# Attention's PSUM banks and the layout of its transposed probabilities, in a hybrid encoder layer

## The chip, the cores and the metric

One core of one Trainium2 chip runs the whole layer as one program. The metric is device time of one execution in microseconds; lower is better. The kernel before takes 2172.15 us, the median of three runs (2170.88 to 2173.38).

## What is computed

One layer over 2048 positions of width 1024. The first half normalises the input, projects it to 1280 columns and splits these among three mixers: a bidirectional diagonal state-space scan (S5), a two-dimensional Fourier mixer, and windowed attention. Their outputs are concatenated, projected, normalised, gated and added to the input. The second half is a gated MLP with a convolution of width 3 between its two products. The change touches attention alone:

```python
def window_attention(q, k, v, sink):
    # 6 query heads, 2 key/value heads of 64; blocks of 128 queries see the 128 keys
    # before, at and after them: kb, vb = band(k), band(v), 384 positions a block
    ...
    scores = jnp.einsum('bnqkgd,bnskd->bnkgqs', qb, kb).astype(jnp.float32) + bias
    ...
    m = jnp.maximum(jnp.max(scores, axis=-1, keepdims=True), sink_l)
    p = jnp.exp(scores - m)
    p = p / (jnp.sum(p, axis=-1, keepdims=True) + jnp.exp(sink_l - m))
    out = jnp.einsum('bnkgqs,bnskd->bnqkgd', p.astype(v.dtype), vb)
    return out.reshape(bsz, seq, ATT_WIDTH)
```

## The kernel before

**Numbers.** Products are made in float16 with each operand split in a high and a low half (HI, LO). A product is then three matmuls: high by high, low by high, high by low (`mm3`). TensorE writes into PSUM, which has eight banks of 128 partitions by 512 float32. The program divides the banks into three pools, `PTAGS`: z has three, s has four, m has one.

**Order of the work.** Every part of the layer is a Python generator. A small planner (`Sched`) runs all of them against modelled clocks: a generator asks for an engine and a duration, or for banks of a pool (`"acq"`), or waits for another's result (`"w"`), and the planner always serves the request that can start first by its model; among those that wait for banks, the one with the lower priority number is looked at first. What comes out is one fixed order of instructions for each engine. On the chip the engines run these orders one instruction after the other; semaphores hold an instruction until its inputs are there. DMAs are issued by SyncE (SP), in order as well. Scratch tiles come from one rotating set of 50 buffers (`u`).

**Who uses which pool around attention.** The S5 chain uses s before attention. The Fourier mixer, the GLU behind S5, the projections of queries (`q_tile`) and the output projection (`proj`) use z. A query tile of chunks 1 to 3 asks for one bank of z with two more to spare, so for a z that is wholly free. The norms' sums over partitions use m. The MLP takes banks of s and z; its first product takes one bank of s as soon as its first weights are there and then waits for its operand.

**Attention** (`att`, L1275 on). The 16 blocks of 128 queries are numbered 0 to 15; four make a chunk of 512 positions (chunks 0 to 3, `c`). Two workers, both instances of the same generator, take the even and the odd blocks, so a pair of blocks (`hb`) is in work at once. Worker 0 loads queries, keys and values of the pair (nine DMAs), once chunk `c`'s query tiles have been stored. The score bank and all other banks of attention come from pool s for chunks 0 and 1, from pool z for chunks 2 and 3 (`bt`). A block goes through these steps:

1. For each of six heads: two score matmuls into a bank, then one VectorE instruction that adds the bias and takes the maximum (L1332).
2. Softmax: maxima with the sink, six exponentials on ScalarE with their sums, reciprocal (L1346) and scale.
3. For each of three pairs of heads: both heads' probabilities are scaled and split into high (ScalarE) and low (VectorE) halves; then they are transposed in 128 by 128 pieces by matmuls against an identity, four pieces to a bank, and each bank is evacuated in one instruction of 512 columns. Of three banks of a pair, ScalarE evacuates two and VectorE one.
4. The output product into one bank: 64 partitions for each of the two value heads, 128 columns for each of its three query heads. As a pair of heads shares a buffer and the middle pair belongs to two value heads, there are four groups of columns: 256, 128, 128 and 256 wide.
5. ScalarE and VectorE evacuate the high and the low half of the output into `ya`, and `f_ya[n]` is set.

**What waits for attention.** The output projection of chunk `c` waits for the four blocks of the chunk. It makes eight tiles of 24 matmuls; each is evacuated by ScalarE twice, once scaled by a constant column (`proj_evac`). Behind it `post` normalises, adds the residual, stores it and prepares the MLP's input. The MLP's first operands are made by `hcomb(0)`, which waits for `f_ya[15]`, the last block.

Nearly all instructions are issued from helpers, so their lines in the profile are the helpers': L318 matmul, L272 ScalarE activation, L277 tensor_tensor, L284 tensor_scalar on VectorE, L291 scalar_tensor_tensor, L267 DMA.

Of the kernel before, what the change touches and what calls it, by code (L numbers as in the profile page):

```python
# [10 lines left out]
F16 = mybir.dt.float16  # L11
I32 = mybir.dt.int32
AF = mybir.ActivationFunctionType
ALU = mybir.AluOpType
X = mybir.AxisListType.X

P = 128
# [20 lines left out]
HI, LO = 0, 1  # L38
# [164 lines left out]
class Builder:  # L203
    UNITS = 50
    PTAGS = {"z": 3, "s": 4, "m": 1}
    LAT = 0.12
    ATT_SLACK = (0.0, 10.0)
    NORM_SLACK = 2.0
    PE_TR = 4
    ATT1 = 0  # L210

    def __init__(self, tc, ctx, A, O):
# [1064 lines left out]
    def att(self, worker):  # L1277

        V, PE, SP = self.V, self.PE, self.SP
        for hb in range(8):  # L1280
            c = hb // 2
            bt = "s" if c < 2 else "z"
            b0, b1 = max(2 * hb - 1, 0), min(2 * hb + 3, 16)
            if worker == 0 and hb % 2 == 0:
                if c == 1 and ATT_GATE:
# [3 lines left out]
            if worker == 0:  # L1289
# [5 lines left out]
                Q, K, VV = self.u([6, 256], F16), self.u([2, 2, 512], F16), self.u([2, 4, P], F16)  # L1295
                t0, nb = hb * 256, b1 - b0
                for x in range(2):
                    for kv in range(2):
                        r = slice(64 * kv, 64 * kv + 64)
                        t = yield from self.dma(ta, Q[64 * x:64 * x + 64, 3 * kv:3 * kv + 3],  # L1300
                                                self.qd[:, r, x, t0:t0 + 256].rearrange("j p t -> p j t"))
                for x in range(2):
                    r = slice(64 * x, 64 * x + 64)
                    for kv in range(2):
                        t = yield from self.dma(ta, K[r, kv, :, :nb * P],
                                                self.kd[:, kv, :, b0 * P:b1 * P].rearrange("x p t -> p x t"))
                t = yield from self.dma(ta, VV[:, :, :nb], self.vd[:, :, b0:b1])
                self.f_q[hb].set(t, (Q, K, VV))
            tq = yield ("w", self.f_q[hb])
            Q, K, VV = self.f_q[hb].val  # L1310
            ya = self.yatt[c]
            n = 2 * hb + worker
            k0, k1 = max(n - 1, 0), min(n + 1, 15)
            nk = k1 - k0 + 1
            bo = (k0 - n + 1) * 128
            st = self.cpool.tile([P, 6, 6], F32, tag="soft", name=self.nm("st"), bufs=4)
            mx, nm, es, r, dn, sm = (st[:, i] for i in range(6))
            sb = []
            tt_ = []
            for h in range(6):  # L1320
                kv = h // 3
                tb = yield ("acq", self.bank[bt], 1)
                ps = self.ps(bt)
                o = ps[:, :nk * 128]
                if h % 2 == 0:
                    sb.append(self.u([2, 384]))
                t = yield from self.mm(max(tb, tq), [(o, Q[:, h, worker * 128:worker * 128 + 128],
                                                      K[:, kv, x, (k0 - b0) * P:(k1 + 1 - b0) * P], x == 0, x == 1)
                                                     for x in range(2)])
                s_ = sb[h // 2][:, h % 2, :nk * 128]  # L1330
                t = yield ("V", 0.08 + 0.00105 * nk * 128, t)
# [4 lines left out]
            t = yield from self.tt(t, mx, mx, self.sink, ALU.max)  # L1336
# [3 lines left out]
            for h in range(6):  # L1340
                s_ = sb[h // 2][:, h % 2, :nk * 128]
                t = yield from self.act(tn, s_, s_, AF.Exp, scale=1.0 / 256, bias=nm[:, h:h + 1],
                                        accum_out=sm[:, h:h + 1])
            t = yield from self.tt(t, dn, sm, es, ALU.add)
            t = yield ("V", 0.1, t)
            V.reciprocal(r, dn)  # L1346
            tr = yield from self.ts(t, r, r, SW, None, ALU.mult)
            pts, tps = [], []
            for g in range(3):
                pp, dd = self.u([2, 2, 384], F16), self.u([2, 2, nk, P], F16)  # L1350
                tp = []
                for j in range(2):
                    h = 2 * g + j
                    s_ = sb[g][:, j, :nk * 128]
                    ph, pl = pp[:, HI, j, :nk * 128], pp[:, LO, j, :nk * 128]
                    t = yield from self.act(tr, ph, s_, AF.Copy, scale=r[:, h:h + 1])
                    t1 = yield from self.stt(t, pl, s_, r[:, h:h + 1], ph, ALU.mult, ALU.subtract)
                    tp.append(t1)
                    if c >= self.PE_TR:
                        for x, src, tx in ((HI, ph, t), (LO, pl, t1)):  # L1360
                            t = yield ("Q", 1.2, tx)
                            SP.dma_start_transpose(out=dd[:, x, j], in_=src)
                        tps_ = t + 2.2 + self.ATT_SLACK[c > 0]
                if c < self.PE_TR:
                    df = dd.rearrange("p x j k q -> p (x j k) q")
                    blk = [(x, j, k) for x in range(2) for j in range(2) for k in range(nk)]
                    for i in range(0, 4 * nk, 4):
                        tb = yield ("acq", self.bank[bt], 1)
                        ps = self.ps(bt)
                        t = yield from self.mm(max(tb, tp[1]), [  # L1370
                            (ps[:, e * P:(e + 1) * P], pp[:, x, j, k * P:(k + 1) * P], self.id16f, True, True)
                            for e, (x, j, k) in enumerate(blk[i:i + 4])])
                        if i % 8 == 0:
                            t = yield from self.act(t, df[:, i:i + 4], ps.rearrange("p (a b) -> p a b", a=4), AF.Copy)
                        else:
                            t = yield from self.ts(t, df[:, i:i + 4], ps.rearrange("p (a b) -> p a b", a=4), 1.0, None, ALU.mult)
                        self.free(t, ps)
                        tps_ = max(t, tps_) if i else t
                pts.append(dd)
                tps.append(tps_)  # L1380
            tb = yield ("acq", self.bank[bt], 1)
            po = self.ps(bt)
            for g, j0, nj in ((0, 0, 2), (1, 0, 1), (1, 1, 1), (2, 0, 2)):
                kv, c0 = divmod(2 * g + j0, 3)
                o = po[64 * kv:64 * kv + 64, c0 * 128:(c0 + nj) * 128].rearrange("p (a b) -> p a b", a=nj)
                cv = slice(64 * kv, 64 * kv + 64)
                t = max(tb, tps[g])
                for k in range(nk):
                    t = yield from self.mm3(t, o, (VV[:, HI, k0 - b0 + k, cv], VV[:, LO, k0 - b0 + k, cv]),
                                            (pts[g][:, HI, j0:j0 + nj, k], pts[g][:, LO, j0:j0 + nj, k]),  # L1390
                                            k == 0, k == nk - 1)
            ql = (n % 4) * 128
            pv = po[:, 0:384].rearrange("p (a b) -> p a b", a=3)
            t = yield from self.act(t, ya[HI][:, :, ql:ql + 128], pv, AF.Copy, scale=1.0 / SW)
            t = yield from self.stt(t, ya[LO][:, :, ql:ql + 128], pv, 1.0 / SW, ya[HI][:, :, ql:ql + 128],
                                    ALU.mult, ALU.subtract)
# [722 lines left out]
```

## Time and profile before

| | |
|---|---|
| median of three runs | 2172.15 us |
| the profiled execution | 2173.84 us |
| its span, first to last instruction | 2172.1 us |
| instructions | 27409 |
| TensorE, VectorE, ScalarE busy | 91%, 72%, 46% of the span |
| mean granted TensorE clock | 0.96 of full speed |
| attention, first score evacuation to last | 466.9 to 839.9 us |

The page of the profile gives busy time by engine, then the span in 40 slices of 54.3 us, in which a digit is a share in tenths. Matmul times overlap, so a busy TensorE is not one at its peak, and the granted clock says at what rate it ran. A row of grouped instructions reads: line, engine, operation, output and inputs, shapes, count, then busy time, mean duration in ns, and the idle time before them with what ended it. A row of the timeline gives start, duration, engine, line, operation and the number of merged instructions. `ps` is a PSUM bank, `u` a scratch buffer, `c` a constant, `st` the softmax columns, `d` a buffer in HBM.

### The profile page before, as it was taken

Reading aid. Unit: us, or ns where it says so; the run is one execution under the profiler, and the core shown is the slowest. Engines: PE = TensorE matmul, PEld = TensorE weight load, DVE = VectorE, ACT = ScalarE, POOL = GpSimd, SP = SyncE. Lnnn points to the kernel's source line nnn. Section 1 sums busy time; section 2 is a strip of 40 time slices with the busy share of each in tenths; the row PEclk is TensorE's granted clock in tenths of the full one; section 3 lists DMA queues with packets and bytes.
Section 4 is the critical chain, followed back from the end, with each engine's and each line's share of the span. In section 5 each row is a group of like instructions: output and inputs, shape, how many; then the busy total and the mean of one; then the engine's idle time right before and its main releaser. Section 6 shows DMA issues by size and latency. Waiting matters only on the chain.

```text
span 2172.1 us, 27409 instructions
## 1 busy us (share of the span) xinstructions
PE 1978.9 (91%) x10072; PEld 989.1 (46%) x10072; DVE 1554.5 (72%) x2291; ACT 1001.2 (46%) x1682; POOL 240.9 (11%) x310
## 2 busy tenths in 40 slices
PE   6788888788997987998999999999999999999997
PEld 1335754444544544443444444444444444444445
DVE  8998898858677566789988884656565664547356
ACT  3643233356567666556655553444444443322321
POOL 1565454002000000000000000000000000011002
PEclk9999999899999988999999999999999999999998
DMA  9362244673747243335655558575757494538533
GB/s 367 107 199 60 59 133 151 219 237 130 253 144 242 79 148 109 128 140 204 243 215 190 188 189 304 173 248 172 247 173 251 137 338 144 180 117 306 183 103 111
DMA packets 206665, 397.31 MB, mean 183 GB/s; under 512 B 19521, under 2 KB 111938, under 8 KB 206530
## 3 DMA queue, kind: packets, MB, share of 16 engines
q1 hardware_dynamic: 206530, 395.55, 52.9%
q8 instruction: 79, 1.29, 0.3%
q14 instruction: 56, 0.46, 0.1%
HBM read 258.93 MB, written 134.98 MB: 181 GB/s over the span
## 4 chain that ended last, share of the span: by engine, by line
PE 53%; DVE 8%; ACT 2%; issue 2%; DMA 0%; POOL 0%; SPq 0%; POOLq 0%; DVEq 0%; ACTq 0%
PE ps L318 53%; DVE u L291 4%; DVE u L277 4%; ACT u L272 2%; DMA u<-d 0%; DVE u L284 0%; DMA d<-u 0%; ACT L272 0%; POOL u L277 0%; DVE u L1332 0%; SPq L267 0%; POOLq L2104 0%; ACT c L272 0%; DVEq L291 0%; DVE st L284 0%
## 5 line engine op out<-in xcount | busy, mean ns | idle before, releaser
L318 PE MATMUL ps<-u,u 128*128 128x512 f16 (+9 forms) x9306 | 1894.1, 364 | 97.6 <-DVE u L291 36.6
L318 PEld LDWEIGHTS <-u 128*128 128x128 f16 (+1 forms) x9334 | 868.2, 100 | 1035.1 <-issue 155.6
L277 DVE TENSOR_TENSOR u<-u,u 128x512 f32<-128x512 f32 (+11 forms) x584 | 508.0, 901 | 105.8 <-ACT u L272 92.1
L272 ACT ACTIVATE u<-u 128x1024 f16<-128x1024 f32 (+7 forms) x485 | 406.3, 869 | 366.9 <-DVE u L277 150.4
L272 ACT ACTIVATE u<-ps 128x512 f32<-128x512 f32 (+7 forms) x511 | 276.9, 555 | 408.2 <-PE ps L318 374.1
L291 DVE SCALAR_TENSOR_TENSOR u<-u,c,u 128x1023 f32<-128x1023 f32 (+5 forms) x248 | 291.1, 1196 | 61.5 <-ACT u L272 54.6
L291 DVE SCALAR_TENSOR_TENSOR u<-ps,u 128x512 f32<-128x512 f32 (+4 forms) x231 | 151.8, 664 | 239.4 <-PE ps L318 200.2
L291 DVE SCALAR_TENSOR_TENSOR u<-u,u 128x1024 f16<-128x1024 f32 (+6 forms) x225 | 240.9, 1092 | 59.1 <-ACT u L272 55.8
L277 POOL TENSOR_TENSOR u<-u,u 128x288 f32<-128x288 f32 (+9 forms) x169 | 183.4, 1099 | 616.0 <-DVE u L291 443.2
L272 ACT ACTIVATE u<-u,c 128x1023 f32<-128x1023 f32 (+3 forms) x106 | 123.5, 1166 | 142.2 <-DVE u L291 122.5
L307 POOL MEMSET u<- 128x1 f32 x88 | 8.6, 98 | 1142.7 <-DVE u L277 395.4
L272 ACT ACTIVATE u<-u,st 128x384 f32<-128x384 f32 (+3 forms) x192 | 109.1, 594 | 35.9 <-DVE st L284 33.5
L318 PEld LDWEIGHTS ps<-u,u 128*128 128x128 f32 (+1 forms) x532 | 92.6, 183 | 43.5 <-DVE u L277 19.7
L318 PE MATMUL ps<-u,c 128*128 128x512 f32 (+4 forms) x142 | 59.2, 533 | 49.9 <-DVE u L302 19.2
L277 DVE TENSOR_TENSOR u<-u 128x512 f32<-128x512 f32 (+8 forms) x136 | 67.3, 499 | 34.1 <-ACT u L272 32.8
L318 PE MATMUL ps<-c,u 128*128 128x128 f16 (+1 forms) x568 | 61.6, 229 | 27.5 <-ACT u L272 16.1
L272 ACT ACTIVATE c<-u 128x2 f32<-128x2 f32 (+1 forms) x88 | 17.8, 203 | 140.0 <-DVE u L291 139.8
L1332 DVE CUSTOM_DVE_ANT_0 u<-ps,u 128x384 f32<-128x384 f32 (+1 forms) x96 | 49.3, 536 | 31.0 <-PE ps L318 30.3
L291 DVE SCALAR_TENSOR_TENSOR u<-u,st,u 128x384 f16<-128x384 f32 (+1 forms) x96 | 55.5, 601 | 18.9 <-ACT u L272 17.9
L302 DVE TENSOR_TENSOR_SCAN u<-u,u 128x512 f32<-128x512 f32 (+1 forms) x60 | 68.3, 1146 | 0.5
L318 PEld LDWEIGHTS ps<-u,c 128*128 128x128 f32 (+1 forms) x142 | 23.0, 182 | 79.4 <-issue 47.4
L272 ACT ACTIVATE u<-u,c,c 128x512 f32<-128x512 f32 (+1 forms) x64 | 48.7, 804 | 19.5 <-DVE c L277 5.7
(52 smaller groups left out, 363.5 us busy)
## 6 DMA issues: line engine op xcount, KB each, us to landing
u<-d SPq DMA_DIRECT2D x226, 512.0 KB
d<-u SPq DMA_DIRECT2D x158, 512.0 KB
d<-u SPq DMA_DIRECT2D x111, 256.0 KB
u<-w_ada SPq DMA_DIRECT2D x48, 512.0 KB
u<-w_up SPq DMA_DIRECT2D x44, 512.0 KB
u<-d SPq DMA_DIRECT2D x66, 256.0 KB
u<-x SPq DMA_DIRECT2D x32, 512.0 KB
u<-d SPq DMA_DIRECT2D x24, 511.0 KB
```

The costliest lines, as they stand in the source:

```text
L272: self.S.activation(out, in_, func, **kw)
L277: (self.V if eng == "V" else self.G).tensor_tensor(out, a, b, op)
L291: self.V.scalar_tensor_tensor(out, a, s, b, op0, op1)
L302: self.V.tensor_tensor_scan(out, d0, d1, 0.0, ALU.mult, ALU.add)
L307: (self.V if eng == "V" else self.G).memset(out, v)
L318: self.PE.matmul(o, a, b, start=st, stop=sp, skip_group_check=chain)
L1332: V.tensor_tensor_reduce(out=s_, in0=o, in1=self.bias[h // 2][:, h % 2, bo:bo + nk * 128], op0=ALU.add, op1=ALU.max, scale=1.0, scalar=-3e ...
```

## The change

All of attention takes its banks from pool s. The six heads are scaled and split first; the transposes come after all of them (`tp` is the latest of the twelve halves). They are gathered by block of keys instead of by pair of heads: one buffer for each key block `k` holds, for each value head, the high and the low half of its three query heads side by side, so 12 pieces in three banks. Evacuations alternate between ScalarE and VectorE over the whole block. The output product then has one group of 384 columns for each value head, in place of four groups in all, and waits key block by key block. A branch for transposes by DMA (`c >= PE_TR`, with `PE_TR` 4 and `c` at most 3) is dropped with its two constants.

```diff
-    ATT_SLACK = (0.0, 10.0)
...
-    PE_TR = 4
...
-            bt = "s" if c < 2 else "z"
+            bt = "s"
...
-            pts, tps = [], []
-            for g in range(3):
-                pp, dd = self.u([2, 2, 384], F16), self.u([2, 2, nk, P], F16)
-                tp = []
-                for j in range(2):
-                    h = 2 * g + j
...
-                    t = yield from self.act(tr, ph, s_, AF.Copy, scale=r[:, h:h + 1])
-                    t1 = yield from self.stt(t, pl, s_, r[:, h:h + 1], ph, ALU.mult, ALU.subtract)
-                    tp.append(t1)
...
-                    for i in range(0, 4 * nk, 4):
-                        tb = yield ("acq", self.bank[bt], 1)
-                        ps = self.ps(bt)
-                        t = yield from self.mm(max(tb, tp[1]), [
-                            (ps[:, e * P:(e + 1) * P], pp[:, x, j, k * P:(k + 1) * P], self.id16f, True, True)
-                            for e, (x, j, k) in enumerate(blk[i:i + 4])])
-                        if i % 8 == 0:
-                            t = yield from self.act(t, df[:, i:i + 4], ps.rearrange("p (a b) -> p a b", a=4), AF.Copy)
-                        else:
-                            t = yield from self.ts(t, df[:, i:i + 4], ps.rearrange("p (a b) -> p a b", a=4), 1.0, None, ALU.mult)
...
+            D, tps, pp, tp = [], [], [], 0.0
+            for h in range(6):
+                g, j = divmod(h, 2)
+                if j == 0:
+                    pp.append(self.u([2, 2, 384], F16))
...
+                t = yield from self.act(tr, ph, s_, AF.Copy, scale=r[:, h:h + 1])
+                t = yield from self.stt(t, pl, s_, r[:, h:h + 1], ph, ALU.mult, ALU.subtract)
+                tp = max(tp, t)
+            blk = [(kv, x, h) for kv in range(2) for x in range(2) for h in range(3 * kv, 3 * kv + 3)]
+            for k in range(nk):
+                D.append(self.u([2, 2, 3, P], F16))
+                df = D[k].rearrange("p v x h q -> p (v x h) q")
+                tps.append(0.0)
+                for i in range(0, 12, 4):
+                    tb = yield ("acq", self.bank[bt], 1)
+                    ps = self.ps(bt)
+                    t = yield from self.mm(max(tb, tp), [
+                        (ps[:, e * P:(e + 1) * P], pp[h // 2][:, x, h % 2, k * P:(k + 1) * P], self.id16f, True, True)
+                        for e, (kv, x, h) in enumerate(blk[i:i + 4])])
+                    src = ps.rearrange("p (a b) -> p a b", a=4)
+                    if (3 * k + i // 4) % 2 == 0:
+                        t = yield from self.act(t, df[:, i:i + 4], src, AF.Copy)
+                    else:
+                        t = yield from self.ts(t, df[:, i:i + 4], src, 1.0, None, ALU.mult)
+                    self.free(t, ps)
+                    tps[k] = max(t, tps[k])
...
-            for g, j0, nj in ((0, 0, 2), (1, 0, 1), (1, 1, 1), (2, 0, 2)):
-                kv, c0 = divmod(2 * g + j0, 3)
-                o = po[64 * kv:64 * kv + 64, c0 * 128:(c0 + nj) * 128].rearrange("p (a b) -> p a b", a=nj)
+            for kv in range(2):
+                o = po[64 * kv:64 * kv + 64, 0:384].rearrange("p (a b) -> p a b", a=3)
                 cv = slice(64 * kv, 64 * kv + 64)
-                t = max(tb, tps[g])
+                t = tb
                 for k in range(nk):
-                    t = yield from self.mm3(t, o, (VV[:, HI, k0 - b0 + k, cv], VV[:, LO, k0 - b0 + k, cv]),
-                                            (pts[g][:, HI, j0:j0 + nj, k], pts[g][:, LO, j0:j0 + nj, k]),
-                                            k == 0, k == nk - 1)
+                    t = yield from self.mm3(max(t, tps[k]), o, (VV[:, HI, k0 - b0 + k, cv], VV[:, LO, k0 - b0 + k, cv]),
+                                            (D[k][:, kv, HI], D[k][:, kv, LO]), k == 0, k == nk - 1)
```

More of the change, by code (lines that the diff above doesn't have):

```diff
@@ L1347, in att @@
             tr = yield from self.ts(t, r, r, SW, None, ALU.mult)
-            pts, tps = [], []
-            for g in range(3):
-                pp, dd = self.u([2, 2, 384], F16), self.u([2, 2, nk, P], F16)
-                tp = []
-                for j in range(2):
-                    h = 2 * g + j
-                    s_ = sb[g][:, j, :nk * 128]
-                    ph, pl = pp[:, HI, j, :nk * 128], pp[:, LO, j, :nk * 128]
-                    t = yield from self.act(tr, ph, s_, AF.Copy, scale=r[:, h:h + 1])
-                    t1 = yield from self.stt(t, pl, s_, r[:, h:h + 1], ph, ALU.mult, ALU.subtract)
-                    tp.append(t1)
[L1359 to L1366, printed above, removed]
-                    for i in range(0, 4 * nk, 4):
-                        tb = yield ("acq", self.bank[bt], 1)
-                        ps = self.ps(bt)
-                        t = yield from self.mm(max(tb, tp[1]), [
-                            (ps[:, e * P:(e + 1) * P], pp[:, x, j, k * P:(k + 1) * P], self.id16f, True, True)
-                            for e, (x, j, k) in enumerate(blk[i:i + 4])])
-                        if i % 8 == 0:
-                            t = yield from self.act(t, df[:, i:i + 4], ps.rearrange("p (a b) -> p a b", a=4), AF.Copy)
-                        else:
-                            t = yield from self.ts(t, df[:, i:i + 4], ps.rearrange("p (a b) -> p a b", a=4), 1.0, None, ALU.mult)
[L1377 to L1380, printed above, removed]
@@ new lines, in att @@
+            D, tps, pp, tp = [], [], [], 0.0
[3 more added lines that the diff above has]
+                    pp.append(self.u([2, 2, 384], F16))
+                s_ = sb[g][:, j, :nk * 128]
+                ph, pl = pp[g][:, HI, j, :nk * 128], pp[g][:, LO, j, :nk * 128]
+                t = yield from self.act(tr, ph, s_, AF.Copy, scale=r[:, h:h + 1])
+                t = yield from self.stt(t, pl, s_, r[:, h:h + 1], ph, ALU.mult, ALU.subtract)
+                tp = max(tp, t)
```

## The prediction

> **What bounds the kernel now.** I read the page first, then busy time by stage, then the chain of waits in order of time.
>
> ```profile
> PE 1978.9 (91%) x10072; PEld 989.1 (46%) x10072; DVE 1554.5 (72%) x2291; ACT 1001.2 (46%) x1682; POOL 240.9 (11%) x310
> ...
> PE   6788888788997987998999999999999999999997
> ...
> PEclk9999999899999988999999999999999999999998
> ```
>
> TensorE is busy 91% of the span, but the average hides two halves. From slice 18 on it is full; before that it is not. Attention's sixteen query blocks lie in slices 8 to 16. The next fence cuts the span where this change cuts the code: the blocks of chunks 0 and 1 (scores already in pool s), those of chunks 2 and 3 (still in pool z), the start of the MLP, and the rest. Columns: length, then busy time of PE, PEld, DVE, ACT, POOL with counts, then the granted clock, DMA share and GB/s.
>
> ```profile
> 467.00:672.00 205.00, 180.11 (x1163) 97.70 (x1163) 154.83 (x345) 129.15 (x272) 16.32 (x15) 0.97 0.54 181
> 672.00:877.00 205.00, 170.62 (x1086) 93.85 (x1084) 129.81 (x283) 129.75 (x273) 0.00 (x0) 0.90 0.42 138
> 877.00:1102.00 225.00, 210.14 (x942) 93.41 (x941) 195.55 (x209) 134.49 (x187) 2.16 (x22) 0.97 0.49 179
> 1102.00:2172.00 1070.00, 1046.02 (x4939) 484.49 (x4938) 670.53 (x725) 421.36 (x636) 32.54 (x86) 0.99 0.57 198
> ```
>
> In the second row no engine is full: PE 170.6 of 205 us, VectorE and ScalarE 130 each, and the clock is only 0.90. That stage is bound by waits between engines, and it is the one whose pool changes. What it loses, the kernel loses: the MLP's first operand waits for the last query block (`f_ya[15]` in `hcomb`), and the last row is nearly pure TensorE work. The chain of waits says the same:
>
> ```profile
> 761.30 5.26 PE ps L318 x36
> ...
> 874.39 59.43 PE ps L318 x262
> ...
> 1102.40 634.08 PE ps L318 x2937
> ```
>
> It runs through the output products of blocks of attention (761.30), then goes straight on from the last block into TensorE work at 874.39. So an attention that ends X us earlier moves nearly X us out of the span, less what VectorE (195.6 of 225 us in the third row) can't follow.
>
> **Where the stage waits.** Blocks 12 and 13 are late. The ScalarE rows below are outputs of block 8 (704.82), block 10 (746.80) and block 11 (766.58); the TensorE rows are first scores: of block 10 (711.62) and of block 12 and 13 (773.04 to 779.54).
>
> ```profile
> 704.82 0.98 ACT L272 ACTIVATE u<-ps 128x384 f16<-128x384 f32 x2 [2.37 <-PE ps L318]
> ...
> 746.80 0.49 ACT L272 ACTIVATE u<-ps 128x384 f16<-128x384 f32 x1
> ...
> 766.58 0.49 ACT L272 ACTIVATE u<-ps 128x384 f16<-128x384 f32 x1 [3.12 <-PE ps L318]
> ```
> ```profile
> 711.62 0.49 PE L318 MATMUL ps<-u,u 128*128 128x384 f16 x2
> ```
> ```profile
> 773.04 1.44 PE L318 MATMUL ps<-u,u 128*128 128x384 f16 x4 [3.65 <-DMA u<-d]
> 777.67 2.07 PE L318 MATMUL ps<-u,c 128*128 128x512 f32 x2 [3.20 <-DVE u L277]
> 779.54 4.10 PE L318 MATMUL ps<-u,u 128*128 128x384 f16 x12
> ```
>
> Block 10 took 711.62 - 704.82 = 6.8 us from its worker's last output to first scores. Block 12 took 779.54 - 746.80 = 32.7 us (its first four matmuls at 773.04 belong to one more pair of heads, the rest stand behind a norm's matmul). Block 13 took 779.54 - 766.58 = 13.0 us. What was it waiting for? Its queries. They come from the third query tile of chunk 3, which needs all three banks of pool z (one plus two spare) and ran here, 12 + 3 + 9 = 24 matmuls:
>
> ```profile
> 750.60 2.75 PE L318 MATMUL ps<-u,u 128*128 128x512 f16 x12
> ...
> 753.64 0.81 PE L318 MATMUL ps<-u,u 128*128 128x512 f16 x3
> ...
> 754.51 2.10 PE L318 MATMUL ps<-u,u 128*128 128x512 f16 x9
> ```
>
> That is right after the projection of chunk 1 let go of pool z. Each projection has eight tiles; the first and the last evacuation of chunks 0, 1 and 2 are:
>
> ```profile
> 576.38 0.67 ACT L272 ACTIVATE u<-ps,c 128x512 f32<-128x512 f32 x1
> ...
> 627.95 0.67 ACT L272 ACTIVATE u<-ps,c 128x512 f32<-128x512 f32 x1
> ...
> 687.83 0.69 ACT L272 ACTIVATE u<-ps,c 128x512 f32<-128x512 f32 x1 [0.41 <-PE ps L318]
> ...
> 747.70 0.68 ACT L272 ACTIVATE u<-ps,c 128x512 f32<-128x512 f32 x1
> ...
> 790.00 0.67 ACT L272 ACTIVATE u<-ps,c 128x512 f32<-128x512 f32 x1
> ...
> 842.17 0.66 ACT L272 ACTIVATE u<-ps,c 128x512 f32<-128x512 f32 x1
> ```
>
> Chunk 0, with attention in the other pool, took 51.6 us; chunk 1, sharing z with attention, 59.9 us; chunk 2, sharing too, 52.2 us. And the queue of SyncE kept the tile's store and the loads behind the residual stores that follow that same projection:
>
> ```profile
> 742.16 0.34 SPq L267 DMA_DIRECT2D u<-d  x1
> 762.40 3.56 SPq L267 DMA_DIRECT2D d<-u  x3
> 766.06 4.64 SPq L267 DMA_DIRECT2D u<-d  x7
> ```
>
> Nothing issues from 742.50 to 762.40; the loads of the queries start at 766.06.
>
> **The change part by part.** Prices of one instruction over the whole run, in the groups kept apart by shape (last numbers: busy us, mean ns):
>
> ```profile
> L291 DVE SCALAR_TENSOR_TENSOR u<-u,st,u 128x384 f16<-128x384 f32 x84 | 50.0, 619 | 18.2 <-ACT u L272 17.2 <-DMA u<-x 0.7
> L272 ACT ACTIVATE u<-u,st 128x384 f16<-128x384 f32 x84 | 47.9, 611 | 3.3 <-issue 1.3 <-DVE st L284 1.1 <-ACT u L272 0.9
> ...
> L272 ACT ACTIVATE u<-ps 128x512 f16<-128x512 f32 x118 | 68.9, 594 | 85.9 <-PE ps L318 85.0 <-DVE u L291 0.4
> ...
> L284 DVE TENSOR_SCALAR u<-ps 128x512 f16<-128x512 f32 x48 | 32.8, 685 | 15.3 <-PE ps L318 15.2
> ```
>
> 1. *Output products.* Per block of three key blocks, 36 matmuls (18 of 256 columns, 18 of 128) become 18 of 384; the columns stay 6912. Block 8's:
>
> ```profile
> 701.82 2.96 PE L318 MATMUL ps<-u,u 128*64 128x256 f16 x36
> ```
>
> 2.96 us over 6912 columns is 0.43 ns a column, and a 512-column stream gives 2.10 us / (9 x 512), 0.46 ns, with its ends. So the short ones already run at the rate of long ones, and I take 0 to 0.1 us a block: at most 1.6 us over 16 blocks; I take 1. The Trainium skill says otherwise (TensorE: Matmul & The Clock Gate, Back-to-back issue gap): in a stream of weight loads and matmuls it gives about 81 ns to one of 128 columns, against 56 ns alone. By that rule, an estimate, 18 x 25 ns or 0.45 us a block and 7 us in all would be saved; the trace doesn't bear it out.
>
> 2. *Evacuations of the transposes.* Number and size stay (nine a block, six at the two edges). The split goes from six on ScalarE and three on VectorE to five and four, so over 14 inner blocks 14 move: ScalarE 14 x 0.594 = 8.3 us less, VectorE 14 x 0.685 = 9.6 us more. VectorE is busy 154.8 + 129.8 of 410 us in the two attention stages, 69%: its idle time hides them. I count nothing; uncovered it would cost up to 9.6 us.
>
> 3. *The barrier of six heads.* Now no transpose starts before all six heads have their high and low halves. Before, the block's longest stretch was ScalarE's, six halves and six evacuations, then a third of the products: 6 x 0.611 + 6 x 0.594 + 0.99 = 8.2 us. Four transposes take
>
> ```profile
> 742.84 0.39 PE L318 MATMUL ps<-c,u 128*128 128x128 f16 x4
> ```
>
> and after the change the stretch is 6 x 0.611, the last low half 0.62, the first transposes 0.39, five evacuations on ScalarE 2.97, and behind the last of them the first value head's last key block (a sixth of 2.96) and the whole second value head (a half), 1.98: 9.6 us. So 1.4 us a block, and for eight blocks one behind the other on each worker 11 us if nothing covers it. Block 10 took 746.80 - 711.62 = 35 us from scores to output, most of it waiting for engines that serve others, so I take a third: 4 us. Ends: 0 and 11.
>
> 4. *The pool.* For chunks 2 and 3 attention leaves z. There the projection and the query tiles stay; in s attention meets only the MLP's first product, which holds one bank while it waits for `f_ya[15]`, so three of the four are left, as many as z had, but not shared. The gain is the hole before blocks 12 and 13. If the third tile still stands behind the projection of chunk 1, that projection ends 59.9 - 51.6 = 8.3 us sooner, and tile, stores and loads with it. If the tile goes ahead of that projection, worker 0's hole shrinks to the 6.8 us of block 10, 26 us less, and worker 1's vanishes but for the 2 us that any start needs: 13.0 - 2 = 11 us, and some 4 us more as its scores no longer stand in one burst with worker 0's (4.10 us at 779.54). The last block is on worker 1, so I count 15. I take this end: while chunk 1's blocks end (around 672) the projection has nothing to do, and what then kept z from being free was block 8's scores. What is late next is the projection of chunk 2, which waits for block 11, and ScalarE's queue.
>
> 5. *Buffers.* Six scratch buffers a block as before, only taken in another order: 0. No DMA is added, and the transposes by DMA that the diff drops were never reached (`c >= 4`).
>
> Sum against the profiled execution's 2173.84 us (span 2172.1 and 1.7 around it): -15 (pool) +4 (barrier) -1 (products) = -12, so 2161.8; the median of the runs is 1.7 below the profiled time, so **2160 us**.
>
> **The rivals.**
>
> *The tile stays behind (B).* Pool z is freed, but the order written by the planner still puts chunk 1's projection first. Then -8.3 + 4 - 1 = -5 us: 2167. For it: the projection asks for one bank where the tile asks for three. Chunk 2's 52.2 us while sharing speaks for still less.
>
> *The barrier decides (C, slower).* Transposes come in one burst after twelve instructions on ScalarE and VectorE, so TensorE, in order, sits before them. In 672 to 877 the granted clock is 0.90, so its idle stretches already cost rate. Should the pool bring nothing, eight rounds cost 11 us less 1 for the products, +10: 2182; with half of the 9.6 us of evacuations on VectorE uncovered, +15. It decides where the interval from a block's reciprocal to its output grows by more than the hole shrinks, 1.4 us a round against 8.3 / 8. The Trainium skill (TensorE: Matmul & The Clock Gate, Part 1: The HAM clock gate) puts a TensorE left idle for about 3.4 us at half its clock. By that rule, each new gap of this length would cost another 1.7 us or so in the window behind it, an estimate; the 0.90 of this stage agrees in kind.
>
> *Nothing to see (D).* Engines' queues, not banks, set attention: the first eight blocks, in s, took the first row's 205 us, and the last eight, in z, the second row's 205. Then 2172 +- 4.
>
> *All holes close (E).* TensorE's whole idle time of the stage, 205 - 170.6 = 34 us, goes: 2138.
>
> **How the numbers follow.** A difference of 0.2% (4.3 us) is about what a measurement can tell here. Chances: the forecast 0.36 and E 0.08 (both faster), B 0.24 (two thirds of it faster by over 4.3 us, a third within), D 0.10 (within, but for a fifth slower), C 0.22. So faster 0.60, same 0.16, slower 0.24. The range, 2133 to 2183, takes in E with a few us for the clock, and C; beyond it stay the full 11 + 10 us of C and mere shifts in the order of work. The forecast's own range, with its pool term between 11 and 26 us and its barrier between 0 and 11, is 2144 to 2172.
>
> **What would show it.** Right: first scores of block 12 within 12 us of block 10's output; third query tile of chunk 3 ahead of the projection of chunk 1; attention's last output near 864 instead of 876; the same 0.43 ns a column in 18 products. B: the tile still follows the projection, which takes about 52 us. C: the reciprocal-to-output intervals grow, TensorE's idle time and low clock in the stage too. Wrong altogether would be a time that moved outside the attention stage, in the first MLP pairs or before 467 us.

## The result and the profile after

The kernel after takes 2139.64 us (median of four, 2133.73 to 2141.87), the kernel before beside it 2172.77: ratio 0.9849, 95% interval 0.983 to 0.9867. It is faster by 33 us, not by the 12 forecast. The profiled execution took 2141.40 us with a span of 2139.6.

The page of the kernel after, the lines shown of before:

```profile
PE 1963.9 (92%) x9796; PEld 967.3 (45%) x9796; DVE 1559.8 (73%) x2305; ACT 991.0 (46%) x1666; POOL 244.6 (11%) x310
...
PE   6788888789988889997999999999999999999997
...
PEclk9989999899999989998999999999999999999998
```

TensorE has 276 matmuls fewer. In both kernels its digits are 9 from slice 19 (counted from 0) to the last but one, but a slice is now 53.5 us and not 54.3. Columns of the next two fences are those of the stage table of the prediction. Kernel before, from the start of the first score evacuation (466.9) to the end of the last block's output evacuation (876.5), and from block 12's first score evacuation on:

```profile
466.90:876.50 409.60, 350.24 (x2245) 191.40 (x2245) 284.23 (x627) 258.90 (x545) 16.32 (x15) 0.93 0.48 160
777.50:876.50 99.00, 80.76 (x498) 43.75 (x499) 63.45 (x142) 65.84 (x138) 0.00 (x0) 0.84 0.37 126
```

Kernel after, between the same two events:

```profile
461.20:839.70 378.50, 335.61 (x1966) 170.58 (x1966) 275.40 (x625) 240.84 (x522) 13.84 (x15) 0.94 0.50 169
768.60:839.70 71.10, 67.87 (x432) 36.55 (x431) 43.11 (x122) 51.09 (x122) 0.00 (x0) 0.98 0.44 144
```

So the attention stage went from 409.6 to 378.5 us, and 28 of these 31 us are in its last stretch, blocks 12 to 15. Its idle time of TensorE fell from 59.4 to 42.9 us and its busy time by 14.6. Around the stage: the first score came 5.7 us sooner, though no instruction ahead of it differs, so this is not the change. (In the nine further kernels with the same order ahead of it the first score came between 456.1 and 464.0.) What follows the stage takes 2172.1 - 876.5 = 1295.6 us before and 2139.6 - 839.7 = 1299.9 after. So the span lost 31.1 in the stage and 5.7 ahead of it, and gained 4.3 behind it: 32.5. (Behind it VectorE, with the norm's work now there, is busy 212.7 of the first 228 us; before it was 195.6 of 225. The prediction had this caveat.) In all eighteen further kernels what follows lies between 1292.9 and 1298.0: nearly a microsecond of the kernel for a microsecond of attention, as forecast. In the chain of waits, after:

```profile
835.37 3.86 PE ps L316 x18
...
839.79 33.84 PE ps L316 x156
...
1067.76 634.07 PE ps L316 x2937
```

the products of the last block are followed, 0.6 us later, by 34 us of TensorE work, and the last full stretch is as long as before (634.07 against 634.08), 35 us sooner.

The holes that the prediction wanted closed: outputs of blocks 8, 10 and 11 in the kernel after are at

```profile
703.77 1.15 ACT L270 ACTIVATE u<-ps 128x384 f16<-128x384 f32 x2 [2.04 <-PE ps L316]
...
738.24 0.49 ACT L270 ACTIVATE u<-ps 128x384 f16<-128x384 f32 x1 [2.28 <-PE ps L316]
...
766.27 0.49 ACT L270 ACTIVATE u<-ps 128x384 f16<-128x384 f32 x1 [3.60 <-PE ps L316]
```

and block 12's first score evacuation, on VectorE, at

```profile
768.63 0.56 DVE L1330 CUSTOM_DVE_ANT_0 u<-ps,u 128x384 f32<-128x384 f32 x1 [1.28 <-PE ps L316]
```

The hole before block 12 is still 768.6 - 738.7 = 29.9 us; by the same two events it was 777.5 - 747.3 = 30.2 before. The query tiles of chunk 3 still come late; the low halves of the second and third are evacuated here:

```profile
748.00 0.69 DVE L289 SCALAR_TENSOR_TENSOR u<-ps,u 128x512 f16<-128x512 f32 x1
756.61 0.69 DVE L289 SCALAR_TENSOR_TENSOR u<-ps,u 128x512 f16<-128x512 f32 x1
```

That is behind the projection of chunk 1, whose eight tiles now lie between

```profile
667.81 0.69 ACT L270 ACTIVATE u<-ps,c 128x512 f32<-128x512 f32 x1 [0.70 <-PE ps L316]
...
714.64 0.70 ACT L270 ACTIVATE u<-ps,c 128x512 f32<-128x512 f32 x1
```

46.8 us instead of 59.9. So the tile did not go ahead of the projection. But z no longer holds it. The last matmuls of the third tile are in the first row below and end at 739.3 (756.6 before). Its high half is evacuated in the third row, behind block 11's first scaling in ScalarE's queue, and its low half at 756.61:

```profile
734.21 5.07 PE L316 MATMUL ps<-u,u 128*128 128x512 f16 x30
...
751.57 0.60 ACT L270 ACTIVATE u<-u,st 128x384 f16<-128x384 f32 x1
752.07 0.58 ACT L270 ACTIVATE u<-ps 128x512 f16<-128x512 f32 x1
...
752.22 0.29 PE L316 MATMUL ps<-c,u 128*128 128x128 f16 x1 [11.59 <-ACT u L270]
...
753.97 2.73 DVE L289 SCALAR_TENSOR_TENSOR u<-u,st,u 128x384 f16<-128x384 f32 x5
```

The fourth row is block 11's first transpose. It starts 0.05 us after the first high half is there, while the last of the low halves ends at 756.70 (fifth row): the barrier is one in the planner's order; on the chip a transpose waits for its own input alone.

What moved is what runs beside blocks 12 and 13. Before, the second norm behind chunk 1's projection scales its eight tiles (`u<-u,c,c`) on ScalarE in the midst of their exponentials (`u<-u,st`, f32):

```profile
791.05 1.51 ACT L272 ACTIVATE u<-u,c,c 128x512 f32<-128x512 f32 x2
792.46 0.61 ACT L272 ACTIVATE u<-u,st 128x384 f32<-128x384 f32 x1
...
793.65 4.33 ACT L272 ACTIVATE u<-u,c,c 128x512 f32<-128x512 f32 x6
```

After, the same eight are done before the first exponential:

```profile
766.66 5.74 ACT L270 ACTIVATE u<-u,c,c 128x512 f32<-128x512 f32 x8
...
775.63 0.62 ACT L270 ACTIVATE u<-u,st 128x384 f32<-128x384 f32 x1 [1.94 <-DVE st L282]
```

The norm behind chunk 2's projection shows the same: before, VectorE spends 13 instructions of about 1.2 us on it from 853.5 to 876.7, in blocks 14 and 15, the first row being one of them; after, it begins only when the last block ends (second row):

```profile
864.77 1.21 DVE L277 TENSOR_TENSOR u<-u,u 128x1024 f32<-128x1024 f32 x1
...
840.25 10.30 DVE L275 TENSOR_TENSOR u<-u,u 128x1024 f32<-128x1024 f32 x9
```

That these norms make the blocks longer is argued from their place in the queues; an experiment below speaks against it as the whole cause. Block 12 took 45.6 us from first score evacuation to output before and 30.0 after, block 15 39.8 and 23.8.

An output product of 18 matmuls, kernel after:

```profile
735.71 2.49 PE L316 MATMUL ps<-u,u 128*64 128x384 f16 x18
```

2.49 us, not 2.9. And the evacuations of transposes moved as counted (ScalarE 118 to 104 of this shape, VectorE 48 to 62):

```profile
L270 ACT ACTIVATE u<-ps 128x512 f16<-128x512 f32 x104 | 60.7, 594 | 74.2 <-PE ps L316 73.5
...
L282 DVE TENSOR_SCALAR u<-ps 128x512 f16<-128x512 f32 x62 | 42.2, 687 | 13.6 <-PE ps L316 13.1
```

### The profile page after: what moved, and what is told of

It is laid out like the page before. It is cut to its first block, busy times and chain, and to the rows that moved or that the text cites. A ratio compares the mean times of both kernels' runs of the same rounds, so it can differ in the third digit from the quotient of the medians.

```text
span 2139.6 us, 26850 instructions
## 1 busy us (share of the span) xinstructions
PE 1963.9 (92%) x9796; PEld 967.3 (45%) x9796; DVE 1559.8 (73%) x2305; ACT 991.0 (46%) x1666; POOL 244.6 (11%) x310
## 4 chain that ended last, share of the span: by engine, by line
PE 49%; DVE 8%; ACT 2%; issue 1%; DMA 1%; POOL 0%; SPq 0%; POOLq 0%; DVEq 0%; ACTq 0%
PE ps L316 49%; DVE u L289 4%; DVE u L275 3%; ACT u L270 2%; DMA u<-d 0%; DMA u<-w_up 0%; DMA d<-u 0%; ACT L270 0%; POOL u L275 0%; SPq L265 0%; POOLq L2095 0%; DVE u L282 0%; ACT c L270 0%; DVEq L289 0%; DVEq L275 0%
## 5 line engine op out<-in xcount | busy, mean ns | idle before, releaser
L316 PE MATMUL ps<-u,u 128*128 128x512 f16 (+5 forms) x9030 | 1879.2, 368 | 90.7 <-DVE u L289 40.5
L316 PEld LDWEIGHTS <-u 128*128 128x128 f16 (+1 forms) x9058 | 846.8, 99 | 1035.4 <-issue 157.6
L275 DVE TENSOR_TENSOR u<-u,u 128x512 f32<-128x512 f32 (+10 forms) x584 | 506.6, 900 | 105.9 <-ACT u L270 92.4
L270 ACT ACTIVATE u<-ps 128x512 f32<-128x512 f32 (+8 forms) x497 | 268.7, 555 | 410.4 <-PE ps L316 377.5
L1330 DVE CUSTOM_DVE_ANT_0 u<-ps,u 128x384 f32<-128x384 f32 (+1 forms) x96 | 48.1, 536 | 23.8 <-PE ps L316 23.7
```

What stands on the lines that cost most here:

```text
L270: self.S.activation(out, in_, func, **kw)
L275: (self.V if eng == "V" else self.G).tensor_tensor(out, a, b, op)
L316: self.PE.matmul(o, a, b, start=st, stop=sp, skip_group_check=chain)
L1330: V.tensor_tensor_reduce(out=s_, in0=o, in1=self.bias[h // 2][:, h % 2, bo:bo + nk * 128], op0=ALU.add, op1=ALU.max, scale=1.0, scalar=-3e ...
```

## The experiments

Times are medians; ratios are to the kernel before on the same chip, which took 2168 to 2170 us in these sets. "Stage" is the time from first score evacuation to last output, each from the kernel's own profile.

| kernel | us | ratio, 95% interval | stage, us |
|---|---|---|---|
| before | 2168 to 2173 | | 409.6 |
| after | 2139.6 | 0.9849 (0.983 to 0.9867) | 378.5 |
| layout alone | 2169.9 | 0.9993 (0.9981 to 1.0005) | 414.4 |
| pool alone | 2164.5 | 0.9970 (0.9959 to 0.9982) | 406.9 |
| after, no barrier | 2158.6 | 0.9944 (0.9925 to 0.9962) | 399.8 |
| after, value heads by turns | 2138.3 | 0.9851 (0.9834 to 0.9868) | 378.8 |
| before, barrier alone | 2166.1 | 0.9985 (0.9975 to 0.9994) | 411.2 |
| after, tiles ask one bank | 2139.5 | 0.9864 (0.985 to 0.9879) | 380.1 |
| before, tiles ask one bank | 2162.5 | 0.9969 (0.9958 to 0.998) | 403.4 |
| after, turns and one bank | 2131.4 | 0.9825 (0.9798 to 0.9852) | 378.0 |
| before, latency 0.13 | 2191.3 | 1.0102 (1.0087 to 1.0117) | 420.1 |
| after, latency 0.13 | 2184.5 | 1.0073 (1.0057 to 1.0088) | 407.2 |
| layout alone, 0.13 | 2181.6 | 1.0054 (1.0029 to 1.0079) | 409.1 |
| pool alone, 0.13 | 2190.3 | 1.0092 (1.0058 to 1.0127) | 416.3 |
| before, latency 0.11 | 2153.8 | 0.9932 (0.9906 to 0.9958) | 400.3 |
| after, latency 0.11 | 2160.3 | 0.9955 (0.9935 to 0.9974) | 406.1 |
| before, score cost +0.02 | 2170.5 | 1.0012 (0.9997 to 1.0027) | 410.5 |
| after, score cost +0.02 | 2140.4 | 0.9876 (0.9827 to 0.9925) | 382.9 |
| before, score cost -0.02 | 2184.0 | 1.0072 (1.0046 to 1.0098) | 424.8 |
| after, score cost -0.02 | 2146.4 | 0.9904 (0.9867 to 0.994) | 391.2 |

**The two parts apart.** Layout alone is the kernel after with

```diff
-            bt = "s"
+            bt = "s" if c < 2 else "z"
```

and pool alone is the kernel before with the opposite edit.

> The kernel after, with chunks 2 and 3 of attention put back into pool z; the layout by key block, the six-head barrier and the wide output products stay. If the pool carries the gain (pool theory, the prediction's), the time returns to 2165 to 2180 us and the last pair of blocks again takes about 98 us from its pair's first score to its last output. If the block's own sequence carries it (layout theory), the time stays at 2135 to 2150. If it is only that the planner's order fell out well (order theory), the time lies anywhere, with chunks 0 and 1 moving too although their pool is the same.

> The kernel before, with all of attention in pool s and nothing else changed. Pool theory: 2135 to 2155 us, with chunks 0 and 1 ending where they did before (block 7 near 672 us). Layout theory: 2165 to 2180. If the two parts add up, the savings of this run and of the layout alone make about 33 us together.

Neither theory holds: the layout alone gives nothing, the pool alone 6 us, both 33. They don't add: with the layout in place the pool is worth 30 us (2169.9 to 2139.6), with the pool in place the layout 25. The stage and its last stretch, layout alone:

```profile
459.10:873.50 414.40, 346.36 (x1966) 172.77 (x1966) 289.03 (x637) 247.10 (x528) 13.83 (x15) 0.92 0.46 157
783.30:873.50 90.20, 73.78 (x429) 37.34 (x428) 55.03 (x134) 51.96 (x121) 0.00 (x0) 0.91 0.37 123
```

and pool alone:

```profile
461.40:868.30 406.90, 353.04 (x2246) 192.83 (x2246) 284.77 (x628) 261.05 (x547) 16.01 (x15) 0.92 0.49 163
772.10:868.30 96.20, 76.79 (x479) 42.76 (x480) 64.20 (x143) 66.43 (x139) 0.00 (x0) 0.85 0.40 134
```

Layout alone ends chunk 1 early too: 189.0 us from the first score to block 7's output, against 206.0 before and 188.0 after. But with attention's blocks in z the query tiles of chunk 3 were evacuated only at 763.7, 768.7 and 772.7 us (after: 729.7, 748.0, 756.6), and blocks 12 to 15 began at 783.3, not 768.6. Pool alone began them at 772.1, but chunk 1 was late (211.0 us), and the norm behind it fell into blocks 12 and 13 as before (scalings at 789 to 795 us). So in this order of work each part seems to remove one of two obstacles.

**The barrier.** The kernel after, with transposes issued pair by pair behind each pair's halves, into the same buffers; and the kernel before with the halves of all six heads first:

```diff
-                    t = yield from self.mm(max(tb, tp), [
-                        (ps[:, e * P:(e + 1) * P], pp[h // 2][:, x, h % 2, k * P:(k + 1) * P], self.id16f, True, True)
-                        for e, (kv, x, h) in enumerate(blk[i:i + 4])])
+            for g in range(3):
...
+                    t = yield from self.mm(max(tb, tp), [
+                        (ps[:, e * P:(e + 1) * P], pp[:, x, h % 2, k * P:(k + 1) * P], self.id16f, True, True)
+                        for e, (x, h) in enumerate(blk)])
```

> The kernel after, in which the transposes of a pair of heads wait for that pair's halves alone and are issued right behind them, pair by pair, into the same buffers by key block. Prediction's step 3: the barrier costs 0 to 11 us, taken as 4, so 2129 to 2140. If instead the burst of transposes behind six heads is what made chunks 0 and 1 faster, taking the barrier away loses up to 20 us: 2145 to 2160.

> The kernel before with one part of the change: all six heads are scaled and split first, then transposed pair by pair; old buffers, old output products, chunks 2 and 3 in pool z. Prediction's step 3: slower by 0 to 11 us. Queue theory (with the barrier ScalarE's scalings no longer stand behind an evacuation that waits for TensorE): from the first score to block 7's output it takes about 188 us as in the kernel after and in the layout alone, not 206; the whole time, as with the layout alone, 2165 to 2172, since chunk 2 starts no earlier for it. If the wide products or the even split of evacuations made chunks 0 and 1 faster, that stretch stays at 206.

Taking the barrier out of the kernel after costs 19 us, though the evacuations into the scattered places take no longer (593 and 686 ns in place of 594 and 687). Put into the kernel before it shortens chunks 0 and 1, to 174.8 us, but not the whole (2166.1): block 8 waits for the third query tile of chunk 2 (low half at 640.3 to 641.0 us), its store and the loads behind it, and starts at 209.7 us after the first score, as late as ever. The time from first score to block 7's output was 169 to 202 us in the eight kernels with the barrier and the planner's settings as they were or with another score cost, with tiles asking for three banks or one, and 206 to 222 in five without it; the sixth, the kernel before whose tiles ask for one bank, took 186.3. From reciprocal to output the first eight blocks took 25.8 us on average before, 19.3 with the barrier alone, 23.4 in the kernel after and 28.1 there without the barrier. Why: without it, an evacuation that waits for TensorE stands in ScalarE's queue ahead of the next pair's scalings. The traces fit that: from the reciprocal to the end of the sixth high half the same blocks, taken in order of time, took 14.4 us before and 16.2 in the kernel after without the barrier, but 6.1 with the barrier alone and 7.3 after. That this alone makes the difference is not shown.

**The products.** The value heads by turns:

```diff
-            for kv in range(2):
...
-                for k in range(nk):
+            for k in range(nk):
+                ops = []
+                for i in range(3):
+                    for kv in range(2):
```

> The kernel after, with the output products of the two value heads issued by turns (first head, second head) instead of one head after the other. In the profile of the kernel after, the products of the two heads overlap for four or five matmuls where one head's follow the other's. If matmuls into the two halves of the columns run beside each other, a block's 18 products take about 1.5 us instead of 2.49; TensorE then saves about 1 us a block, and the time falls by 0 to 10 us (2130 to 2140). If the overlap is only in how the trace models ends, the products keep 2.4 to 2.9 us and the time stays within 4 us of 2140.

A block's 18 products take 1.65 us, starts of a pair 3 ns apart: TensorE is busy 325.8 us in the stage, 10 less than after. The time stays (2138.3 against 2139.6), as does the stage:

```profile
464.00:842.80 378.80, 325.79 (x1966) 166.09 (x1966) 276.37 (x626) 241.23 (x522) 13.79 (x15) 0.92 0.50 167
```

What the products gave up turned into idle time of TensorE, 53.0 us of it.

**The query tiles.**

```diff
-        ps, t = yield from self.ztile(wf.val, wf.t, c, 2 if c else 0, fh=fh)
+        ps, t = yield from self.ztile(wf.val, wf.t, c, 0, fh=fh)
```

> The kernel after, in which a query tile of chunks 1 to 3 asks for one bank of pool z instead of for all three. Tile theory (what is left of the holes before blocks 8 and 12, 628 to 676 and 739 to 768 us in the kernel after, is query tiles waiting for a free z): both holes shrink to 7 to 15 us and the time falls by 15 to 40 us, to 2100 to 2125. Theory that the holes are filled with work that must be done anyway: the holes move, the time stays within 8 us of 2139.

> The same with the kernel before: query tiles ask for one bank. Tile theory: the hole before block 12 shrinks from 33 us to about 7 and the time falls by 10 to 30 us (2140 to 2160) with attention still in pool z. Other theory: within 8 us of 2170.

The tiles of chunk 3 now come at 590 to 611 us, block 8 starts 169.8 us after the first score instead of 214.4, and the hole before block 12 is 5.6 us. The stage of the kernel after stays at 380.1 us:

```profile
462.60:842.70 380.10, 338.29 (x1965) 170.93 (x1964) 279.89 (x630) 250.98 (x530) 14.63 (x15) 0.94 0.49 166
```

So the holes, on which the prediction rests, don't set the length; in the kernel before, closing them gave 6 us (2162.5). Nor does the place of the norms alone. In the kernel after with this edit the scalings of the norm behind chunk 2's projection stand among block 13's high halves (789.7 to 797.1 us), and VectorE does four products of 1.2 us beside them:

```profile
793.01 0.60 ACT L270 ACTIVATE u<-u,st 128x384 f16<-128x384 f32 x1
793.51 0.20 ACT L270 ACTIVATE st<-st 128x6 f32<-128x6 f32 x1
793.61 1.51 ACT L270 ACTIVATE u<-u,c,c 128x512 f32<-128x512 f32 x2
```

The stage holds the same TensorE work in every kernel so far (301 to 302 us of float16 columns at 512 in 214 ns, as in these traces), and work that no longer waits in one place waits in another. Even so, before and after differ by 23 us with this edit in both.

**How much is the order.** Two nudges that change no instruction, only the planner's model: its latency, which shifts all of the kernel, and the modelled cost of a score instruction, which moves nothing ahead of attention.

```diff
-    LAT = 0.12
+    LAT = 0.13
...
-                t = yield ("V", 0.08 + 0.00105 * nk * 128, t)
+                t = yield ("V", 0.10 + 0.00105 * nk * 128, t)
```

> The kernel before, with the planner's modelled latency 0.13 in place of 0.12: the same instructions in a slightly other order. Order theory (a good part of any of these differences is how the order falls out): the time moves by 8 us or more either way. Else it stays within 4 us of 2170.

> The kernel after with the planner's modelled latency 0.13 in place of 0.12: the same instructions in another order. The same step moved the kernel before from 2169 to 2191 us. If the 33 us belong to the change, this kernel stays 20 to 45 us under the kernel before at the same setting (2146 to 2171). If they are luck of the order, it lies within 10 us of 2191 or above.

> Layout alone (chunks 2 and 3 in pool z) at latency 0.13. At 0.12 it changed nothing. If the two parts only work together, it lies within 8 us of 2191 again; if the layout has a gain of its own that the order hid, 2160 to 2180.

> Pool alone (old layout, all attention in pool s) at latency 0.13. At 0.12 it saved 6 us. If the two parts only work together, 2178 to 2191; if the pool has a gain of its own that the order hid, 2155 to 2175.

> The kernel after at latency 0.11. If the attention stage of this kernel is robust against the order, as three orders of it say (378 to 380 us from first score to last output), the stage takes 370 to 390 us here and the whole 2130 to 2150. If those three were luck, it lies anywhere up to 2180.

> The kernel before at modelled latency 0.11, to be set beside the kernel after at 0.11 (2160 us). If the change carries about 30 us whatever the order: 2180 to 2195. If the order carries most: 2155 to 2172.

> The kernel after, with the planner's modelled cost of a score instruction 0.02 us higher; nothing ahead of attention moves. Change theory: 2130 to 2150, as in the three orders with a stage of 379 us. Order theory: anywhere from 2135 to 2175.

> The kernel before under the same nudge. Change theory: 2160 to 2180. Order theory: anywhere from 2145 to 2185.

> The kernel after with that modelled cost 0.02 us lower. Change theory: 2130 to 2150; order theory: 2135 to 2175.

> The kernel before, with the planner's modelled cost of a score instruction 0.02 us lower. Change theory: 2160 to 2180, 20 us or more above the kernel after under the same nudge. Order theory: anywhere from 2145 to 2185.

With latency 0.13 the kernel before loses 22 us and the kernel after 45; with 0.11 they gain 15 and lose 21. There the change is worth -7 and +6.5 us, and the stage of the kernel after is 407 and 406 us:

```profile
474.10:881.30 407.20, 344.36 (x1999) 176.21 (x1998) 270.69 (x618) 237.00 (x519) 6.34 (x6) 0.92 0.45 152
```

With the score cost nudged it is worth -30 and -38 us. Over the six pairs (as it stands -33, one bank -23, latency -7 and +6.5, score cost -30 and -38) the mean is -21. In the four pairs whose order is the same up to 440 us, the change is worth 23 to 38. Over all kernels at latency 0.12, the six with both the barrier and pool s for all blocks have a stage of 378 to 391 us, the eight with one of them or neither 400 to 425. So in these orders the gain needs the two together, and another order can take it all away. Whether it needs the wide products too is not shown: no kernel has the two with the old products. What in the order at 0.11 and 0.13 does so stays open; there chunk 1 starts later in three of the four kernels (block 4's first score 138 to 158 us after the first, against 90 to 96 in both kernels as they stand), and chunks 0 and 1 are longer with the barrier than without (252 against 236 us, 232 against 219).

**Both edits joined.**

> The kernel after with the products of the two value heads by turns and with query tiles that ask for one bank. Each alone left the time at 2138 to 2140 us. If the stage is bound by the chain of a block through ScalarE and VectorE, 2125 to 2145; if holes and TensorE's work stood in for each other in those two runs, both gone give 2100 to 2125.

At 2131.4 us it lies below both kernels; its interval overlaps that of the kernel after. The stage is 378.0 us as in the others, so the last 8 us are not shown to come from it: its first score was early (457.8).

## Why the prediction was wrong

The direction held, and so did the frame: attention is the stage, what follows it hardly changes, and its gain passes nearly one to one. The size failed, by step 3's sign and by adding up parts that don't add; step 4's mechanism failed too.

- *The pool (step 4), -15.* Its mechanism failed. It says "I take this end", that the third tile goes ahead of chunk 1's projection and the hole before block 12 closes. It did not: tile behind the projection, hole 30 us as before, now for the tile's evacuations in the queues. The pool alone measured -6, about its other end, rival B's -8.3; with the new layout it measured -30. And the runs with tiles that ask for one bank show that closing the hole isn't worth its length.
- *The barrier (step 3), +4.* The step that made the size wrong: without the barrier the kernel after is 19 us slower. It has a wait that isn't there, "no transpose starts before all six heads have their high and low halves": on the chip the first transpose of 14 of the 16 blocks starts before the last low half is there, block 11's with the first high half. And it summed one block's longest stretch as if its engine were its own. In the run, two workers and a projection share each queue, and the reciprocal-to-output interval fell (25.8 to 23.4 us, with the barrier alone to 19.3) where the sum had it rise by 1.4. With -19 in place of +4 the sum would be -35, near the measured -33; but that is luck, as the parts don't add.
- *The products (step 1), -1.* 0.47 us a block, 7.5 in all, not 0 to 1.6. That 128-column matmuls cost hardly more per column was right (56 ns apart in the trace of before, 256-column ones 109); the saving comes from the seam between the two value heads, where their matmuls overlap, and more so when they are wide. In time even 0.84 us more a block gave 1 us. The Trainium skill's rule (TensorE: Matmul & The Clock Gate, Back-to-back issue gap) gave about the right saving, 0.45, by luck: the 81 ns on which it rests don't appear.
- *Evacuations (step 2) and buffers (step 5), 0.* 14 moved at the prices given, and nothing in the stage shows a cost.
- *What no step had.* The parts work together only (0, -6, and -33 for both), and the order that the planner writes is worth more than any term: a nudge of its model moved the kernel before by -15 to +22 us. The range, 2133 to 2183, held the result; the sum was made as if the order stood still around the edit.

Of the rivals, C is refuted, and so is D; B is right that the tile stays behind the projection and wrong on the time; E's 34 us nearly came, but only half of them (16.5) out of TensorE's idle time in the stage.

## What to carry to other kernels

When a planner orders the work, price an edit over several orders: nudge a modelled cost in both kernels and compare pairs, since one pair mixes the edit with luck. A hole in a queue is worth its length only if nothing that fills it is missed elsewhere; check that by closing the hole alone. In queues that are shared and in order, try putting instructions that wait for nobody ahead of those that wait for another engine; here it was worth 19 us in one order of work, while at the other two latencies chunks 0 and 1 were longer with it.

## What the runs showed of the hardware

Matmuls whose outputs are 64 partitions each, in different halves of one bank's partitions, run beside each other. With the two value heads one after the other, 384-column matmuls start 162 ns apart, and only some four or five at the seam overlap (18 in 2.49 us); by turns they start in pairs 3 ns apart, 162 ns from pair to pair, 18 in 1.65 us. It is no matter of modelled ends: by turns, the evacuation that waits for the products of one block starts 1.7 us after the first of them starts, and 2.5 with the heads one after the other.
